# Two decoder layers in float32: gate and up by seven products of half size, and inner tiles in groups of six

## The chip, the core and the metric

The kernel runs on one core of one Trainium2 chip. A core has engines with an instruction queue each: TensorE (PE) multiplies matrices into banks of PSUM, of which this kernel uses eight, 128 x 512 numbers each; VectorE (DVE), ScalarE (ACT) and GpSimd (POOL) work on tiles of 128 partitions in on-chip memory (SBUF); SyncE (SP) issues the DMAs that bring data from HBM. Engines run side by side and wait for each other by semaphores. The metric is the time of one execution on the device in microseconds, the median of several runs.

## The reference

Two layers on x of 512 tokens by 1024, float32. Each layer is an FFN, a token mixer and an FFN:

```python
h = _rmsnorm(x) * (1.0 + sc1) + sh1
x = x + HALF_STEP * g1 * (jax.nn.silu(h @ w_gate) * (h @ w_up)) @ w_down
h = _rmsnorm(x) * (1.0 + sc2) + sh2
x = x + g2 * _hybrid_mixer(h, w_in[l], w_out[l], ...)
h = _rmsnorm(x) * (1.0 + sc3) + sh3
x = x + HALF_STEP * g3 * _swiglu(h, ffn2 weights)
```

`w_gate` and `w_up` are 1024 x 2816, `w_down` is 2816 x 1024. The shifts, scales and gates (sh, sc, g) are nine rows per layer, `SiLU(c) W_mod + b_mod`: one token's vector times 1024 x 9216 weights. The mixer has projections (1024 x 3584), three kinds of attention and an output projection; the change leaves its arithmetic alone.

## The kernel before, in words

**Layout and precision.** Everything is held transposed: features in partitions, the 512 tokens in columns. A block is 128 features; h has 8 blocks (`ND`), the inner width 22 tiles (`NF`). The products run on operands of the type fp32r. Each operand is split exactly into two parts of 12 bits, a high part (a cast on ScalarE) and a low part (VectorE subtracts the cast from the original), and each product is three matmuls, high x high, high x low, low x high: `triple` (L742). Matmuls add up in a PSUM bank over the blocks.

**FFN** (`ffn`, L848). Inner tiles go in groups of 8, 8 and 6 (L851). In a group they go by pairs: one load of 1 MB holds the 1024 x 256 weights of gate for two tiles, the next those of up. For each tile `dense` (L818) runs 8 blocks x 3 parts = 24 matmuls of 512 columns into one bank. ScalarE takes SiLU of a gate's bank (`gate_out`), VectorE multiplies by the up bank, and the result is split into high and low hidden rows (`up_out`). After the group's last tile come its down products (`down`, L911): for each of 8 output blocks, the group's inner tiles x 3 matmuls, added to x by VectorE (`residual`). The first pair of an FFN runs half the tokens at a time (`first`, L825), because h comes in halves from `norm` (L748). The first FFN's first pair has a hand-written order (`opening`, L338). At the end of an FFN the last four output blocks also go in halves.

**Weights** (`feed`, L703). `plan` (L603) lists all loads in order; SP's queue issues each as soon as one of three buffers (`RAW`) is free. A weight load is split by two casts and two subtractions of 128 x 1024 elements into the pools `WH` and `WL`, two of each. Among the weights, `plan` puts 64 loads of modulation weights, 1 MB each: one or two after each pair of tiles, one after each load of down weights. VectorE multiplies and adds them up (`background`, L645: two operations of 1024 elements per load, and a reduction after every fourth).

**Order.** The order in each engine's queue is fixed when the program is built. Streams of steps (main, feed, background, one per bank to be emptied) are merged by `Flow` (L143): of all steps that may run, the one goes next that a plain model of the engines would start first, with small biases. Slots of SBUF and banks are handed out in that order. The banks are in two pools, `M` (2) and `B` (6). Every instruction is recorded through one helper (L104), so the profile shows nearly all under that line and is read by the tiles' names: `m` and `a` are the banks of `M` and `B`, `w` a loaded buffer, `wh` and `wl` its parts, `hh` and `hl` the parts of h, `u` any of the 42 slots, `x` the residual stream, `acc` the modulation's sums.

Of the kernel before, what the change touches and what calls it, by code (L numbers as in the profile page):

```python
# [11 lines left out]
F32 = mybir.dt.float32  # L12
# [81 lines left out]
class Engine:  # L94
    """An engine that tells the Flow what each instruction reads, writes and about takes."""
# [19 lines left out]
class Pool:  # L115
    """Slots of one tag: how many are held, and about when each free one was last used."""
# [15 lines left out]


class Step:
    """What a stream does next: on which engine, after which tiles, with how many new slots."""
# [7 lines left out]
class Flow:  # L143
    """Emits streams of instructions (generators of Steps) merged into one program order.

    Of all streams whose next step may run, the one goes first that a plain model of the engines
    would start first; between equals the one of the higher rank.
    """
# [4 lines left out]
    def __init__(self):  # L153
        self.clk = dict.fromkeys(("PE", "ACT", "DVE", "POOL", "SP"), 0.0)
        self.ready, self.used, self.writer, self.owner = {}, {}, {}, {}
        self.streams, self.serial = [], 0
# [21 lines left out]

    def account(self, eng, op, out, ins):
        if eng == "SP":  # L180
# [3 lines left out]
            n = out.tensor.name  # L184
            start = max(self.clk["SP"], 0.0 if self.writer.get(n) == "SP" else self.ready.get(n, 0.0))
            self.clk["SP"] = start + size / 350e3
            end = self.clk["SP"] + 2.0
        else:
            t = self.clk[eng]
            for a in [out, *ins]:  # L190
                n = a.tensor.name
                if a.space != bass.MemoryType.DRAM and self.writer.get(n) != eng:
                    t = max(t, self.ready.get(n, 0.0))
# [3 lines left out]
        for a in ins:  # L197
            self.used[a.tensor.name] = max(self.used.get(a.tensor.name, 0.0), end)
        n = out.tensor.name
        self.used[n] = max(self.used.get(n, 0.0), end)  # L200
        if eng == "PE":
            end = max(end, self.ready.get(n, 0.0))
        self.ready[n] = end
        self.writer[n] = eng
# [16 lines left out]
    def start(self, s):  # L221
# [3 lines left out]
        for pool, n in st.need:  # L225
            if len(pool.free_at) < n + st.spare:
                return None
        t = self.clk[st.engine] if st.engine != "SP" else self.clk["PE"]
        late = self.MARGIN if st.engine == "PE" and s[0] == 0 else LATE if st.engine == "PE" and s[0] == 4 else 0.0
        for a in st.deps:  # L230
            t = max(t, self.ready.get(a.tensor.name, 0.0) + late)
# [22 lines left out]
def trunk(ctx, tc, x, c, w_mod, b_mod, f1g, f1u, f1d, w_in, w_out, qng, kng, hng, lbl, f2g, f2u, f2d, cf, out):  # L254
# [13 lines left out]
    U = Pool(F, space("up", UNITS), "u", [P, S], UNITS)  # L268
    RW = Pool(F, space("wraw", RAW), "w", [P, 8, 256], RAW)
    WH = Pool(F, space("whi", SPLIT), "wh", [P, 8, 256], SPLIT)  # L270
    WL = Pool(F, space("wlo", SPLIT), "wl", [P, 8, 256], SPLIT)
    HH = Pool(F, space("hhi", ND), "hh", [P, S], ND)
    HL = Pool(F, space("hlo", ND), "hl", [P, S], ND)
# [64 lines left out]
    def opening():  # L338
        """Up to the products of the first tiles of gate and up, in a fixed order.

        Layer 0's first shift and scale come 256 columns of each at a time, and are followed by the
        products of the two rows of h that they give.
        """
        hs = [(HH.get(F32R), HL.get(F32R)) for _ in range(ND)]
# [49 lines left out]
        def row_sums(e, n):  # L394
            """The first n rows' share of the modulation, on the tensor engine."""
# [38 lines left out]
        tmp = [U.get() for _ in range(3)]  # L434

        def modulate(d):
            hi, lo = hs[d]
            t = tmp[d % 3]
# [8 lines left out]
        def products(which, ds):  # L447
            for d in ds:
                for i in range(2):
                    w, o = ws[which], slice(i * P, (i + 1) * P)  # L450
                    triple(outs[2 * which + i], w[0][:, d, o], w[1][:, d, o], *hs[d], d == 0, d == ND - 1)

        def split(r, engine):
            hi, lo = WH.get(F32R), WL.get(F32R)
            ws.append((hi, lo))
            for h in range(2):
                cs = slice(h * P, (h + 1) * P)
                A.copy(hi[:, :, cs], r[:, :, cs])
                engine.tensor_sub(lo[:, :, cs], r[:, :, cs], hi[:, :, cs])
# [33 lines left out]
        U.put(junk, *tmp)  # L493
# [4 lines left out]
        return hs, outs  # L498
# [37 lines left out]
    def lower_bounds():  # L536
        """Of both layers side by side: [lower bound of layer 0 | of layer 1], four columns each."""
# [38 lines left out]
        # near 1 the logarithm is 2 atanh((v - 1) / (v + 1))  # L576
# [24 lines left out]
    MODS = [(0, j) for j in (2, 4, 3, 5, 7, 6, 8)] + [(1, j) for j in (1, 0, 2, 4, 3, 5, 7, 6, 8)]  # L601

    def plan():  # L603
# [6 lines left out]
        def through(l, j):  # L610
            """All modulation up to the one named."""
# [3 lines left out]
        for l in range(DEPTH):  # L615
            for wg, wu, wd, last in ((f1g, f1u, f1d, 0), (f2g, f2u, f2d, 1)):
                for f0 in range(0, NF, 8):
                    n = min(8, NF - f0)
# [939 lines left out]
```

## Time and profile before

| | before |
|---|---|
| median of 3 runs | 2170.38 us (2168.68 to 2173.84) |
| profiled execution, its span | 2173.2 us |
| TensorE busy | 2127.0 us, 98% |
| weight loads into TensorE busy | 1809.0 us, 83% |
| VectorE busy | 1237.3 us, 57% |
| ScalarE busy | 808.6 us, 37% |
| GpSimd busy | 177.9 us, 8% |
| DMA | 259.06 MB, 119 GB/s mean |

The profile is of one execution. Its span, from the first to the last instruction, is what it gives of that execution's own time. A group's row gives line, engine, operation, tile written <- tiles read, shape and count, then busy time and mean duration in ns, then the engine's idle time before it and what ended that. Busy time is the union of instructions, so where they overlap at their ends it counts once, while the mean is of whole durations. A timeline row gives start, length, and how many instructions of a kind were merged into it (x2). Pieces of the chain of work that ended last are given as start, length, engine and tile, count. The two layers show as FFN 0 (to about 380 us), mixer, FFN 1 (from about 745), FFN 2 (from about 1108), mixer, FFN 3 (from about 1808).

### The profile page before, as it was taken

The numbers are of one execution on the slowest core, as the hardware profiler recorded it, in microseconds if no ns is written. First come the engines' busy times: TensorE is split into PE (matmuls) and PEld (weight loads), VectorE is DVE, ScalarE is ACT, GpSimd is POOL, SyncE is SP. The second block draws the span as 40 slices with busy tenths as digits, with TensorE's granted clock in tenths as the row PEclk, the third lists the DMA queues.
The fourth block names the chain that finished last, engine by engine and source line by source line (L and its number), as shares of the span: only waits on it lengthen the run. The fifth ranks groups of instructions, "written<-read, shape, count | busy, mean of one in ns | idle before, by whom it ended". The sixth has DMA issues, their size and how long they took to land.

```text
span 2173.2 us, 26686 instructions
## 1 busy us (share of the span) xinstructions
PE 2127.0 (98%) x10936; PEld 1809.0 (83%) x10936; DVE 1237.3 (57%) x1874; ACT 808.6 (37%) x1272; POOL 177.9 (8%) x219
## 2 busy tenths in 40 slices
PE   7999999999999999999999999999999999999999
PEld 6888888988887888888898888888878788888887
DVE  5765554675678665455475546447766866333333
ACT  3332222465655432222342222236464644222221
POOL 3000000140320100000000000003013201000000
PEclk7999999999999999999999999999989999999999
DMA  8555453221111155454335545432101113223221
GB/s 293 187 205 194 155 174 117 97 79 59 50 42 65 59 190 190 135 173 152 130 103 170 180 150 174 150 102 98 59 26 62 49 59 117 97 97 97 97 83 54
DMA packets 206625, 259.06 MB, mean 119 GB/s; under 512 B 4927, under 2 KB 188186, under 8 KB 206504
## 3 DMA queue, kind: packets, MB, share of 16 engines
q1 hardware_dynamic: 206472, 257.33, 35.3%
q8 instruction: 86, 1.41, 0.3%
q14 instruction: 35, 0.29, 0.0%
q0 software_dynamic: 32, 0.04, 0.0%
HBM read 255.25 MB, written 2.10 MB: 118 GB/s over the span
## 4 chain that ended last, share of the span: by engine, by line
PE 93%; DVE 4%; ACT 1%; issue 1%; DMA 0%; POOL 0%; SPq 0%; POOLq 0%; DVEq 0%; ACTq 0%
PE m L104 59%; PE a L104 34%; DVE wl L104 1%; DVE u L104 1%; ACT u L104 1%; DVE hl L104 1%; DVE acc L104 1%; ACT wh L104 0%; DVE x L104 0%; DMA u<-in_x_dram 0%; POOL u L104 0%; SPq L104 0%; ACT hh L104 0%; ACT L104 0%; ACT x L104 0%
## 5 line engine op out<-in xcount | busy, mean ns | idle before, releaser
L104 ACT CAST wh<-w 128x1024 fp32r<-128x1024 f32 (+1 forms) x348 | 344.8, 1018 | 744.8 <-PE m L104 542.8
L104 DVE TENSOR_TENSOR wl<-w,wh 128x1024 fp32r<-128x1024 f32 (+1 forms) x346 | 416.0, 1225 | 253.7 <-ACT wh L104 250.1
L104 PE MATMUL m<-u,wh 128*128 128x512 f32 (+1 forms) x1808 | 514.7, 370 | 3.6 <-DVE u L104 2.3
L104 PE MATMUL m<-hh,wh 128*128 128x512 f32 (+1 forms) x1072 | 415.3, 387 | 4.2 <-DVE x L104 4.1
L104 PE MATMUL m<-hl,wh 128*128 128x512 f32 (+1 forms) x1072 | 406.0, 379 | 2.5 <-DVE hl L104 2.4
L104 PE MATMUL m<-hh,wl 128*128 128x512 f32 (+1 forms) x1072 | 405.6, 378 | 0.5 <-DVE wl L104 0.5
L104 PEld LDWEIGHTS m<-u,wh 128*128 128x128 f32 x1808 | 324.1, 189 | 60.7 <-DVE u L104 3.6
L104 PE MATMUL m<-u,wl 128*128 128x512 f32 (+1 forms) x904 | 331.4, 367 | 0.0
L104 PE MATMUL a<-hh,wh 128*128 128x512 f32 (+1 forms) x816 | 302.6, 371 | 0.0
L104 PE MATMUL a<-hh,wl 128*128 128x512 f32 (+1 forms) x816 | 302.3, 370 | 0.1
L104 PE MATMUL a<-hl,wh 128*128 128x512 f32 (+1 forms) x816 | 301.9, 370 | 0.0
L104 PEld LDWEIGHTS m<-hh,wh 128*128 128x128 f32 x1072 | 206.6, 193 | 38.9 <-ACT u L104 4.6
L104 PEld LDWEIGHTS m<-hl,wh 128*128 128x128 f32 x1072 | 206.3, 192 | 37.9 <-DVE hl L104 3.9
L104 PEld LDWEIGHTS m<-hh,wl 128*128 128x128 f32 x1072 | 205.4, 192 | 38.5 <-DVE wl L104 1.4
L104 POOL TENSOR_TENSOR u<-u 128x256 f32<-128x256 f32 x162 | 126.2, 806 | 1260.4 <-ACT u L104 1246.5
L104 DVE SCALAR_TENSOR_TENSOR x<-m,mod,x 128x512 f32<-128x512 f32 (+1 forms) x136 | 91.0, 671 | 212.1 <-PE m L104 212.0
L104 DVE TENSOR_TENSOR u<-u 128x256 f32<-128x256 f32 (+3 forms) x324 | 185.6, 593 | 37.9 <-ACT u L104 34.7
L104 PEld LDWEIGHTS m<-u,wl 128*128 128x128 f32 x904 | 171.0, 189 | 28.1
L104 PEld LDWEIGHTS a<-hh,wl 128*128 128x128 f32 x816 | 154.7, 190 | 26.5 <-DVE wl L104 0.3
L104 PEld LDWEIGHTS a<-hl,wh 128*128 128x128 f32 x816 | 154.7, 190 | 25.8
L104 PEld LDWEIGHTS a<-hh,wh 128*128 128x128 f32 x816 | 154.5, 189 | 25.6
L104 DVE TENSOR_TENSOR u<-u,a 128x512 f32<-128x512 f32 x88 | 60.2, 687 | 196.7 <-PE a L104 196.0
(132 smaller groups left out, 2054.4 us busy)
## 6 DMA issues: line engine op xcount, KB each, us to landing
w<-in_w_mod_dram SPq DMA_DIRECT2D x64, 1024.0 KB, 4.7
w<-in_ffn_w_gate_dram SPq DMA_DIRECT2D x44, 1024.0 KB, 5.2
w<-in_ffn_w_up_dram SPq DMA_DIRECT2D x44, 1024.0 KB, 5.2
w<-in_ffn_w_down_dram SPq DMA_DIRECT2D x32, 1024.0 KB, 5.1
w<-in_w_in_dram SPq DMA_DIRECT2D x28, 1024.0 KB, 5.0
w<-in_ffn_w_down_dram SPq DMA_DIRECT2D x16, 768.0 KB, 5.3
u<-in_w_mod_dram SPq DMA_DIRECT2D x32, 256.0 KB, 6.6
w<-in_w_out_dram SPq DMA_DIRECT2D x8, 512.0 KB, 4.0
```

The source lines that it names most:

```text
L104: ins = fn(*args, **kw)
```

## The change

Gate and up of nine pairs of tiles in each FFN (tiles 4 to 21; the first two pairs stay as they were) are computed by a scheme with seven products where the plain one has eight. The work of one load, 1024 x 256 weights times 1024 x 512 of h, is cut in two each way: the blocks of h into 4 and 4, the 256 columns into two tiles, the tokens into two halves. Each of the seven products is 4 blocks x 3 parts of 256 columns. Their operands are quarters of h and of the weights, and sums of such quarters.

- `feed` makes the weights' sums from a load of kind "f": four additions of 128 x 512 elements in place, then four parts a, b, c, d (1024, 512, 1024 and 1024 elements) cast and subtracted. They take 7 slots of 4 KB, out of 11 that weights may hold (`HELD`); 4 slots are a plain load's share.
- `combine` makes the sums of h once per FFN from values that `norm` keeps: per block, four operations of 256 elements, two casts and two subtractions of 512.
- `seven` issues the products into three banks. Four of them go to the first bank and add up on what it holds; ScalarE copies the bank's state out between them (`empty`), VectorE does three operations of 256 elements. SiLU and the product with up are then taken in halves for one tile of the pair, whole for the other (`gate_seven`, `up_seven`).
- Groups are of 6, 6, 6 and 4 inner tiles, so there are four rounds of down products and of adding to x, not three; modulation loads come after every second load of down weights.
- Slots: one pool of 37 slots of 4 KB (`Slots`), whole or as two halves of one type, serves h, weights and all else, in place of separate pools. Plain loads are split by blocks (0 to 3, 4 to 7), not by columns.
- `Flow` follows halves of a slot apart.

The core of the diff (comments and docstrings also go):

```diff
-UNITS = 42
+SLOTS = 37
 RESERVE = 4
 RAW = 3
-SPLIT = 2
+HELD = (11, 8)
+GROUP = 6
+FAST = (tuple(range(4, NF, 2)),) * 4
...
                         if f or not (l or last):
                             yield from take(2 if f < TWO[2 * l + last] else 1)
...
-                        yield from take(1 if n == 8 else 0)
+                        yield from take(1 if n == GROUP and dd % 4 == 0 else 0)
...
+            elif item[0] == "f":
+                w = {}
+                r0, r1 = r[:, 0:4], r[:, 4:8]
+                c0, c1 = slice(0, P), slice(P, 2 * P)
+                yield Step("ACT", r, need=((WS, 2),), bias=haste())
+                w["a"] = hi, lo = [WS.get().rearrange("p (k f) -> p k f", f=P) for _ in range(2)]
+                A.copy(hi, r[:, :, c0])
...
+                A.copy(b[:, 0], r1[:, :, c1])
...
+                V.tensor_sub(lo, r[:, :, c0], hi)
...
+                V.tensor_add(r0[:, :, c0], r0[:, :, c0], r0[:, :, c1])
...
+                V.tensor_sub(b[:, 1], r1[:, :, c1], b[:, 0])
...
+                V.tensor_add(r0[:, :, c1], r0[:, :, c1], r1[:, :, c1])
+                for n, rr in (("c", r0), ("d", r1)):
+                    yield Step("ACT", r, need=((WS, 2),), bias=haste())
+                    w[n] = hi, lo = [WS.get().rearrange("p (k f) -> p k f", f=256) for _ in range(2)]
+                    A.copy(hi, rr)
+                    if n == "c":
+                        yield Step("DVE", r, bias=haste())
+                        V.tensor_add(r1[:, :, c1], r0[:, :, c0], r1[:, :, c1])
+                        yield Step("DVE", r, bias=haste())
+                        V.tensor_add(r1[:, :, c0], r1[:, :, c1], r1[:, :, c0])
+                    yield Step("DVE", hi, bias=haste())
+                    V.tensor_sub(lo, rr, hi)
...
+    QUARTER = {"w11": ("a", 0, 0), "w21": ("a", 4, 0), "w22": ("b", 0, 0), "t1": ("c", 0, 0), "t3": ("c", 0, P),
+               "t4": ("d", 0, 0), "t2": ("d", 0, P)}
+    def seven(w, hs, sums, banks, uid):
...
+        for n, a, q, bank, begin, after, free in (
+                (1, (0, 0), "w11", 0, True, (), ""), (5, "x5", "t1", 2, True, (), ""), (6, "x6", "t2", 0, False, ("s1",), ""),
+                (2, (0, 1), "w21", 1, True, (), "a"), (7, "x7", "t3", 0, False, ("s2",), "c"),
+                (3, "x3", "w22", 2, False, ("s5",), "b"), (4, (1, 1), "t4", 0, False, ("s7",), "d")):
+            if after:
+                yield when(*((uid, z) for z in after))
+            ps = banks[bank][:, :HALF]
+            for k in range(4):
+                wh, wl = quarter(q, k)
+                xh, xl = rows(a, k)
+                yield Step("PE", xl, wh, wl)
+                triple(ps, wh, wl, xh, xl, begin and k == 0, k == 3, True)
...
+    def empty(banks, uid, fin):
...
+        A.copy(e0[:, lo], b0)
+        done.add((uid, "s1"))
...
+        A.copy(e1[:, hi], b2)
+        done.add((uid, "s5"))
...
+        A.copy(e1[:, lo], b0)
+        done.add((uid, "s2"))
...
+        V.tensor_add(e0[:, lo], e0[:, lo], b1)
...
+        A.copy(e0[:, hi], b0)
+        done.add((uid, "s7"))
...
+        V.tensor_sub(e1[:, hi], e1[:, hi], e0[:, hi])
...
+        V.tensor_sub(e1[:, lo], b2, e1[:, lo])
...
+                if f in fast:
+                    yield when((phase, "sums"))
+                    for name, pools, fin in (("g", (M, M, B), gate_seven), ("u", (B, B, B), up_seven)):
+                        w = yield from next_weight()
+                        yield Step("PE", need=tuple((p, pools.count(p)) for p in (M, B) if p in pools))
+                        banks = [p.get() for p in pools]
+                        uid = (phase, name, f)
+                        F.spawn(empty(banks, uid, fin(f)), 0)
+                        yield from seven(w, hs, sums[phase], banks, uid)
```

More of the change, by code (lines that the diff above doesn't have):

```diff
@@ L131, in put, with room, __init__, whole @@
             heapq.heappush(self.free_at, self.flow.used.get(t.tensor.name, 0.0))
+    def room(self, n, spare):
+        return len(self.free_at) >= n + spare
+class Slots:
+    def __init__(self, flow, pool, n):
+        self.flow, self.pool, self.free_at = flow, pool, [0.0] * n
+        self.open = {F32: [], F32R: []}
+        self.parents = {}
+    def whole(self, dt=F32R):
+        t0 = heapq.heappop(self.free_at)
+        t = self.pool.tile([P, 2 * S], dt, tag="u", name="u")
+        n = t.tensor.name
+        self.parents[n] = t
+        self.flow.halved.add(n)
+        for i in range(2):
+            self.flow.ready[n, i] = t0
+        return t
+    def get(self, dt=F32):
+        if self.open[dt]:
+            self.open[dt].sort(key=lambda h: h[0])
+            _, t, i = self.open[dt].pop(0)
+            self.flow.ready[t.tensor.name, i] = max(self.flow.ready[t.tensor.name, i], self.flow.used.get((t.tensor.name, i), 0.0))
+        else:
+            t, i = self.whole(dt), 0
+            self.open[dt].append((self.flow.ready[t.tensor.name, 1], t, 1))
+        return t[:, i * S:(i + 1) * S]
+    def pair(self):
+        t = self.whole()
+        return t[:, :S], t[:, S:]
+    def put(self, *tiles):
+        for t in tiles:
+            n, used = t.tensor.name, self.flow.used
+            for k in self.flow.keys(t):
+                i = k[1]
+                spot = self.open[t.dtype]
+                other = [h for h in spot if h[1].tensor.name == n]
+                if other:
+                    spot.remove(other[0])
+                    heapq.heappush(self.free_at, max(used.get((n, 0), 0.0), used.get((n, 1), 0.0)))
+                else:
+                    spot.append((used.get(k, 0.0), self.parents[n], i))
+    def room(self, n, spare):
+        one = len(self.open[F32]) if n == 1 else 0
+        n += spare
+        return 2 * len(self.free_at) + one >= n + (n % 2 if not one else 0)
+class Held:
+    def __init__(self, slots, most):
+        self.slots, self.most, self.n = slots, most, 0
+    def get(self):
+        self.n += 1
+        return self.slots.whole()
+    def put(self, *tiles):
+        self.n -= len(tiles)
+        self.slots.put(*tiles)
+    def room(self, n, spare):
+        return self.n + n <= self.most and len(self.slots.free_at) >= n + spare
 class Step:
@@ L177, in cost, with keys @@
         return 0.0
+    def keys(self, a):
+        n = a.tensor.name
+        if n not in self.halved:
+            return (n,)
+        o = a.offset % (2 * S)
+        e = o + sum(step * (count - 1) for step, count in list(a.ap)[1:])
+        return tuple((n, i) for i in range(o // S, e // S + 1))
     def account(self, eng, op, out, ins):
@@ L225, in start @@
         for pool, n in st.need:
-            if len(pool.free_at) < n + st.spare:
+            if not pool.room(n, st.spare):
                 return None
@@ L738, in release, with part @@
     def release(w):
-        WH.put(w[0])
-        WL.put(w[1])
-    def triple(ps, wh, wl, xh, xl, start, stop):
-        T.matmul(ps, wh, xh, start=start, stop=False)
-        T.matmul(ps, wh, xl, start=False, stop=False)
-        T.matmul(ps, wl, xh, start=False, stop=stop)
-    def norm(phase, l, jsh, t, hs, order):
+        for parts in w:
+            WS.put(*parts)
+    def part(w, k, i=None):
+        o = slice(0, 256) if i is None else slice(i * P, (i + 1) * P)
+        return tuple(z[:, k % 4, o] for z in w[k // 4])
```

310 lines of the change are left out of this document (226 added, 84 removed).

## The prediction

> **What bounds the kernel now.** Read first: the page's busy times, then its slices, then the chain of work that ended last.
>
> ```profile
> span 2173.2 us, 26686 instructions
> PE 2127.0 (98%) x10936; PEld 1809.0 (83%) x10936; DVE 1237.3 (57%) x1874; ACT 808.6 (37%) x1272; POOL 177.9 (8%) x219
> DVE  5765554675678665455475546447766866333333
> PEclk7999999999999999999999999999989999999999
> PE 93%; DVE 4%; ACT 1%; issue 1%; DMA 0%; POOL 0%; SPq 0%; POOLq 0%; DVEq 0%; ACTq 0%
> ```
>
> Matmul ends are modelled, so 98% alone proves little; but 93% of the chain lies on TensorE, its granted clock is full outside the opening, and only 46 us of the span (2173.2 - 2127.0) show no matmul. TensorE is the bound nearly everywhere. VectorE is next: 50 to 80% busy in most slices, 30% in the last FFN.
>
> What a matmul costs is read from pieces of the chain (start, duration, count) where nothing but matmuls stands:
>
> ```profile
> 895.44 10.88 PE m L104 x48
> 752.80 5.76 PE m L104 x48
> ```
>
> The first is one weight load's work, a pair of tiles of a gate: 2 tiles x 8 blocks x 3 parts = 48 matmuls of 512 columns, 10.88 / 48 = 227 ns each. The second is the start of a phase, where half the tokens go at a time: 256 columns, 5.76 / 48 = 120 ns each. Every matmul has its own weight load in both. Half the columns cost 53% of the time.
>
> **The products.** Per weight load the change replaces 48 x 227 ns = 10.88 us by 7 products x 4 blocks x 3 parts = 84 x 120 ns = 10.08 us: 0.80 us less. There are 9 pairs x 2 (gate, up) x 4 FFNs = 72 such loads, all on the path: **-57.6 us**.
>
> The Trainium skill (TensorE: Matmul & The Clock Gate, "Back-to-back issue gap") puts the gap at N/2.4 + 2.5 ns, 109 and 216 ns here, by which this term would be an estimated -86 us. The trace's 120 and 227 ns differ from it by some 11 ns on either, which is lost on every half-width matmul, and they decide.
>
> **What VectorE gets for it.** Its prices, from pairs that run back to back and from groups:
>
> ```profile
> 918.14 2.36 DVE L104 TENSOR_TENSOR wl<-w,wh 128x1024 fp32r<-128x1024 f32 x2 [0.21 <-ACT wh L104]
> 1826.55 1.28 DVE L104 TENSOR_TENSOR u<-u,a 128x512 f32<-128x512 f32 x2
> 469.42 0.74 DVE L104 TENSOR_TENSOR u<-u 128x256 f32<-128x256 f32 x2
> 899.56 2.60 DVE L104 SCALAR_TENSOR_TENSOR acc<-w,sc_c,acc 128x1024 f32<-128x1024 f32 x2
> L104 DVE TENSOR_TENSOR wl<-w,wh 128x1024 fp32r<-128x1024 f32 x298 | 368.5, 1261 | 229.0 <-ACT wh L104 225.4
> L104 DVE TENSOR_TENSOR u<-u,a 128x512 f32<-128x512 f32 x88 | 60.2, 687 | 196.7 <-PE a L104 196.0 <-ACT u L104 0.7
> L104 DVE SCALAR_TENSOR_TENSOR acc<-w,sc_c,acc 128x1024 f32<-128x1024 f32 x112 | 143.5, 1281 | 2.0
> L104 DVE TRANSPOSE_TENSOR_REDUCE p<-acc 128x32 f32<-128x1024 f32 x16 | 19.9, 1244 | 0.5
> L104 DVE SCALAR_TENSOR_TENSOR mod<-a,bcol 32x8 f32<-32x8 f32 x64 | 10.3, 161 | 24.1 <-PE a L104 23.4
> ```
>
> Instructions overlap at their ends: a second one adds 2.36 - 1.26 = 1.10 us (1024 elements), 1.28 - 0.69 = 0.59 (512), 2.60 - 1.28 = 1.32 (modulation's sum); for 256 I take half a pair, 0.37. Per pair of tiles:
> - Splitting a load: two subtractions (2.2 us) become three of 1024, one of 512 and four additions of 512: 3 x 1.10 + 5 x 0.59 = 6.25. Gate and up: 12.5.
> - Emptying the banks: new, three operations of 256 per load, 2 x 3 x 0.37 = 2.2.
> - Multiplying by up, splitting the hidden rows: 0.59 + 2 x 0.37 + 2 x 0.59 = 2.5.
>
> That is 17.2 us against TensorE's 2 x 10.08 = 20.16. A modulation load adds 2 x 1.32 + (1.24 + 4 x 0.16) / 4 = 3.1. With one per pair, VectorE needs 20.3 us of 20.16. It is not yet the bound, because work can be done ahead. A full group of three pairs with three modulation loads needs 51.6 + 9.3, and 1.7 for the first down weights: 62.6. While the group before ends, one whole load (6.25) and the first part of the next (1.10 + 3 x 0.59 = 2.9) fit into the 11 slots; about 2 us fall behind the group's end. That leaves 51.5 of 60.5 us, 85%; in FFN 0's second group, with five modulation loads, 57.7, 95%. The down products give the room ahead:
>
> ```profile
> 829.90:873.40 43.50, 43.50 (x194) 36.01 (x194) 24.51 (x28) 8.37 (x9) 0.00 (x0) 1.00 0.56 188
> 1826.80:2160.00 333.20, 333.20 (x1483) 275.76 (x1482) 124.92 (x140) 85.08 (x105) 0.00 (x0) 1.00 0.29 96
> L104 DVE SCALAR_TENSOR_TENSOR x<-m,mod,x 128x512 f32<-128x512 f32 x96 | 71.8, 751 | 191.7 <-PE m L104 191.6
> w<-in_w_mod_dram SPq DMA_DIRECT2D x64, 1024.0 KB, 4.7
> w<-in_ffn_w_gate_dram SPq DMA_DIRECT2D x44, 1024.0 KB, 5.2
> ```
>
> In a group's down products (columns of a window: length, then PE, PEld, DVE, ACT, POOL) VectorE works 24.5 of 43.5 us. With six inner tiles they take 32.7 us, need 8 x 0.75 for residuals, 4 x 1.7 for weights and two modulation loads, 19 us, and leave 13 free for the 9.1 above. The last FFN, at 125 of 333 us, has room everywhere. Two more things I cost at nothing: the 8 residuals more per FFN (6 us, in those 13; uncovered, 24 in all) and the sums of x (4 blocks x (4 x 0.37 + 2 x 0.59) = 11 us per FFN), which have the first two pairs, 43 us, before their first use (uncovered, 44 in all). On SP's queue the modulation loads move: two per group of down weights, not four. Each issue waits for a free buffer, with the next weights behind it. A buffer is now held for the length of a load's products, 10 us: two loads of 5.2 + 10 and one of 4.7 + 3 are 38 of the 3 x 20 us that three buffers offer per pair, so the queue keeps up; with two modulation loads 46.
>
> I still expect weights to come late at times. Part c of the next load gets its slots when 4 of the 7 products of this one are done, at 5.8 us; a cast (1.0, half of the row of 2.01 below), two additions and a subtraction make 9.1, and it is asked for at 10.1 + 1.44 = 11.5. Part d follows at 10.2 for 13.0. So 2.4 us are spare, and a modulation step (1.32) with one subtraction (1.10) in the way uses them. I take 0.2 us for each of the 54 loads in the first three FFNs: **+11**, bounds 0 and the second rival.
>
> **Ends of groups.** The last product now finishes both tiles, so hidden tile k = n - 2 is late where it was one tile (5.4 us) early.
>
> ```profile
> L104 PE MATMUL a<-hl,wh 128*128 128x256 f32 x160 | 45.3, 283 | 0.0
> L104 DVE TENSOR_TENSOR u<-u 128x256 f32<-128x256 f32 x132 | 56.9, 468 | 6.8 <-ACT u L104 6.8
> L104 ACT CAST u<-u 128x512 fp32r<-128x512 f32 x102 | 62.9, 618 | 157.9 <-DVE u L104 157.7
> L104 DVE TENSOR_TENSOR u<-u 128x512 fp32r<-128x512 f32 x136 | 95.7, 709 | 29.0 <-ACT u L104 27.2 <-POOL u L104 1.2
> ```
>
> From the last matmul's start: 0.28 + 0.37 + 0.47 (two halves multiplied) + 0.62 + 0.71 = 2.45 us. The down products ask for that tile after 0.12 + 4 x 3 x 0.227 = 2.84 us in a group of six, after 1.48 in the last group of four. With nothing in the queues: 12 groups at 0, 4 at 1.0. With two weight subtractions in the way (2.2): 12 x 1.8 + 4 x 3.2 = 34. I take half a one at each of two steps: 12 x 0.6 + 4 x 1.5 = **+13**, bounds 4 and 34.
>
> **Bank reuse.** Four products add up in one bank, which ScalarE reads in between; one product on another bank, 12 x 0.120 = 1.44 us, covers each read.
>
> ```profile
> 301.30 2.01 ACT L104 CAST wh<-w 128x1024 fp32r<-128x1024 f32 x2 [9.15 <-PE m L104]
> L104 ACT COPY u<-m 128x256 f32<-128x256 f32 x8 | 3.0, 374 | 8.6 <-PE m L104 8.3
> ```
>
> 0.28 + 0.37 = 0.65 us of 1.56 (with the last matmul's own 0.12); one cast in the way (about 1.0) just uses the rest. **+4** for 216 reads, bounds 0 and the third rival. Opening, mixers and changes of phase keep their work; the new order and pool of slots may move their 46 us without matmuls by -5 to +8; I take 0.
>
> **Sum:** -57.6 + 11 + 13 + 4 = -29.6: 2173.2 becomes 2143.6 in the profiled execution, which was 2.8 above the median of 2170.4; by the median **2141 us**, with its own bounds at 2120 and 2160.
>
> **Rivals.**
> 1. *Everything stays covered.* VectorE's 85% with 9 us done ahead speaks for it, the 95% group against. Only the four short groups cost 4: 2170.4 - 57.6 + 4 = 2117, to 2112 with what the mixers may give.
> 2. *Slower: VectorE's order holds the gate and up stage.* Before, a group of three pairs took 3 x 21.76 = 65.3 us; VectorE needs 51.5. If waits between it and ScalarE let it use less than 51.5 / 65.3 = 79% of the stage, the group loses. For it: no FFN slice of before shows VectorE at 80%. Against: it idled then because it had nothing to do. At 75% a group lasts 68.7 (+3.4), that with five loads 76.9 (+11.6); with the short groups at +1: FFN 0 +16, the next two +8 each, the last FFN -12: +20, 2190; at 70% 2230.
> 3. *Bank reads held up.* Two casts ahead of a copy cost 0.65 + 2.0 - 1.56 = 1.1 us; at every fifth of 216 reads 47 us, so -57.6 + 13 + 47: 2173, no change. For it: per load, casts and copies go from 2.0 to 3 x 1.0 + 0.62 + 4 x 0.37 = 5.1 of 10.1 us, and a cast that waits for a slot or for VectorE holds every copy queued behind it, and so TensorE. Against: that is still half. The Trainium skill (Perfetto Trace Analysis, "Matmuls") advises rotating independent groups through banks and larger matmuls; this change goes against both, and no row of before shows the cost.
> 4. *TensorE's own weight loads lie open,* 36 more of them per load of 1 MB:
>
> ```profile
> L104 PEld LDWEIGHTS a<-hh,wl 128*128 128x128 f32 x816 | 154.7, 190 | 26.5 <-DVE wl L104 0.3
> ```
>
> At 190 ns a matmul 84 x 0.190 = 16.0 us, 72 x 5.1 = 367 us slower, 2537. The 120 ns above, loads included, speak against it. The Trainium skill (TensorE: Matmul & The Clock Gate, "The mechanism") lets a load overlap running matmuls only where row groups differ; the trace disagrees, by 120 against 190 ns.
>
> **How the numbers follow.** Forecast 0.56, first rival 0.19, second 0.16, third 0.08, fourth 0.01. Two runs of this kernel can be told apart from about 0.2%, 4.3 us. Faster: 0.56 + 0.19 + 0.01 of the third = 0.76; same: 0.05 of it; slower: 0.19. The range runs from the first rival into the second, 2114 to 2186; some 0.06 lies below and 0.12 above.
>
> **What would show it.** Right: matmul pieces of x84 or so at 10.1 us in the gates and ups of all FFNs; VectorE about 85 to 95% in the first three FFNs' gate and up; TensorE's gaps 1 us long, at the starts of down products, and behind the splitting of weights where modulation runs; the last FFN shorter by some 10 us. Wrong: 256 columns at other than 120 ns; TensorE idle 2 us and more per load behind VectorE (second rival) or behind ScalarE's copies (third); a mixer that is longer.

## The result, and the profile after

The changed kernel takes 2220.68 us (median of 4 runs, 2218.92 to 2222.76) where the kernel before takes 2169.53 beside it: a ratio of 1.0225, with a 95% interval of 1.0206 to 1.0243. It is slower by 2.2%; the forecast was faster, 2141 us. In the profiled executions the span goes from 2173.2 to 2221.0 us, +47.8.

From the page of the kernel after: its span, the engines' busy times, the slices of VectorE and of the granted TensorE clock, and the chain that ended last.

```profile
span 2221.0 us, 33173 instructions
...
PE 2101.4 (95%) x13456; PEld 1896.7 (85%) x13456; DVE 1679.5 (76%) x2694; ACT 1048.2 (47%) x1797; POOL 191.7 (9%) x221
...
DVE  6778788678558787878878778878755878776765
...
PEclk7889999999899999999999999999999999999999
...
PE 82%; DVE 11%; DMA 3%; ACT 2%; issue 1%; SPq 0%; ACTq 0%; DVEq 0%
```

There are more matmuls (13456, before 10936), and TensorE's busy time falls by 25.6 us where the products alone should have given 57.6, so the other matmul time grew by 32 us. About 20 of them are the clock: TensorE is busy for 116 us of stretches with a granted clock of 0.5, before for 76, and half of such a stretch is lost (summed over both traces). The other 12 I can't put down to one cause. The time without a matmul grows from 46.2 to 119.6 us (2221.0 - 2101.4). So +47.8 is -57.6, +32.0 of other matmul time and +73.4 without any. VectorE's share of the chain rises from 4% to 11%.

Where this lies is seen in windows cut at the same places of the two kernels' FFNs (length; busy time and count of PE, PEld, DVE, ACT, POOL; granted clock, DMA share, GB/s). First the kernel before, FFN 0, 1 and 3:

```profile
0.00:439.40 439.40, 420.72 (x2021) 356.65 (x2022) 260.35 (x366) 144.28 (x211) 26.09 (x25) 0.96 0.52 176
...
764.20:1131.70 367.50, 365.16 (x1768) 309.41 (x1767) 198.95 (x242) 108.67 (x150) 7.66 (x10) 1.00 0.45 152
...
1826.70:2173.20 346.50, 341.68 (x1524) 282.38 (x1522) 128.59 (x145) 85.12 (x105) 0.00 (x0) 1.00 0.29 94
```

The kernel after, FFN 0, 1 and 3:

```profile
0.00:491.30 491.30, 426.46 (x2642) 386.12 (x2643) 367.48 (x566) 205.32 (x343) 29.24 (x26) 0.91 0.47 155
...
816.80:1186.70 369.90, 356.61 (x2390) 328.67 (x2389) 304.00 (x447) 168.00 (x281) 8.86 (x10) 0.99 0.44 143
...
1874.80:2221.00 346.20, 332.26 (x2172) 303.74 (x2170) 241.53 (x347) 138.99 (x229) 0.00 (x0) 0.98 0.32 101
```

FFN 0 with the opening is 51.9 us longer, FFN 1 2.4 longer, FFN 2 0.5 and FFN 3 0.3 shorter; by the sum each should have been 6 to 10 us shorter. (The mixers make up the rest: +0.7 and -6.4.) The clock fell in FFN 0 above all, from 0.96 to 0.91.

The products themselves do what was forecast. From the chain of the kernel after, in FFN 3 (start, length, what):

```profile
1990.50 10.08 PE a L109 x84
...
2010.66 10.09 PE a L109 x84
...
2020.77 0.43 DVE u L109 x2
...
2021.45 2.52 DVE u L109 x3
...
2024.01 1.19 PE m L109 x4
```

84 matmuls take 10.08 us, one load's work. Behind the last of a group the chain goes over VectorE to the last hidden tile, 3.3 us later, while TensorE has down products of the other tiles to do: this group's down products take only 0.6 us more than their matmuls. Where modulation runs, the same 504 matmuls of a group (six loads) look like this, in windows of the kernel after: FFN 0's second and third group, FFN 1's third, and FFN 3's second for comparison.

```profile
178.60:252.30 73.70, 66.65 (x509) 65.25 (x508) 55.93 (x81) 33.38 (x58) 0.00 (x0) 0.93 0.38 126
285.40:354.30 68.90, 64.20 (x508) 62.95 (x508) 60.38 (x87) 33.65 (x61) 0.00 (x0) 0.95 0.45 148
990.60:1060.10 69.50, 64.46 (x508) 63.32 (x507) 60.42 (x87) 33.65 (x61) 0.00 (x0) 0.95 0.45 147
1960.10:2020.60 60.50, 60.50 (x506) 60.50 (x505) 46.75 (x70) 32.92 (x60) 0.00 (x0) 1.00 0.28 89
```

The last row is the ideal, 60.5 us with TensorE busy throughout, VectorE 46.75. The third groups of FFN 0 and FFN 1 took 69 us, and VectorE has 60.4 us of work in them, as much as TensorE would have needed. The second group of FFN 0 took 73.7 with VectorE at work for only 55.9. That looks like another cause, and the rows behind it show which. DMA issues of SP there, then VectorE, then TensorE (start, length, what, idle before it and what ended that):

```profile
190.05 0.37 SPq L109 DMA_DIRECT2D w<-in_ffn_w_up_dram  x1
192.69 10.10 SPq L109 DMA_DIRECT2D w<-in_w_mod_dram  x2
210.84 0.37 SPq L109 DMA_DIRECT2D w<-in_ffn_w_gate_dram  x1
```

```profile
209.59 1.22 DVE L109 TENSOR_TENSOR u<-w,u 128x1024 fp32r<-128x1024 f32 x1
...
216.90 0.42 DVE L109 TENSOR_TENSOR u<-u,a 128x256 f32<-128x256 f32 x1 [4.49 <-PE a L109]
217.24 1.28 DVE L109 SCALAR_TENSOR_TENSOR acc<-w,sc_c,acc 128x1024 f32<-128x1024 f32 x1
...
233.45 1.28 DVE L109 SCALAR_TENSOR_TENSOR acc<-w,sc_c,acc 128x1024 f32<-128x1024 f32 x1
```

```profile
223.91 0.50 PE L109 MATMUL a<-u 128*128 128x256 f32 x2 [1.36 <-ACT u L109]
226.11 2.50 PE L109 MATMUL a<-u 128*128 128x256 f32 x10 [1.70 <-DVE u L109]
```

Three buffers take loads. At 202.8 two hold modulation's loads (the second row is two issues, the last at 202.42) and one an up load. The next gate's load has to wait until the split of that up load ends at 209.59 + 1.22 = 210.81; it is issued at 210.84. VectorE meanwhile idles for 4.49 us, until a bank of TensorE is ready; the first sum of the load issued at 192.69, which had long landed (5.1 us by the median of its queue), stands behind that in VectorE's order and runs at 217.24, the second at 233.45. So this load keeps a buffer for 42 us. When the gate is there, its split starts late, and TensorE waits 1.36 and 1.70 us for its parts. From issue to the end of its second sum, where it gives up the buffer, a modulation load takes 18.6 us before and 31.1 us after (mean of the 64 loads, each issue of SP with the pair of sums on `acc` that belongs to it, in the order of both); the prediction had 4.7 + 3.

The start of FFN 3's down products shows what TensorE makes of it. VectorE, then TensorE:

```profile
1924.35 1.83 DVE L109 TENSOR_TENSOR u<-w,u 128x1024 fp32r<-128x1024 f32 x2 [1.35 <-ACT u L109]
1926.10 2.60 DVE L109 SCALAR_TENSOR_TENSOR acc<-w,sc_c,acc 128x1024 f32<-128x1024 f32 x2
1928.73 1.25 DVE L109 TRANSPOSE_TENSOR_REDUCE p<-acc 128x32 f32<-128x1024 f32 x1
```

```profile
1930.03 0.63 PE L109 MATMUL a<-p,quads 128*128 128x32 f32 x2 [4.78 <-DVE p L109]
1932.62 9.74 PE L109 MATMUL m<-u 128*128 128x512 f32 x29 [1.95 <-DVE x L109]
```

Modulation's last sums stand between the splits of down weights that came late, and TensorE, whose queue holds modulation's closing product (`p`, `quads`), waits 4.78 us for it and 1.95 us for x behind it. Then it is slow for a while, as windows behind the gap show:

```profile
1932.60:1939.30 6.70, 6.68 (x17) 5.26 (x18) 0.53 (x1) 0.55 (x2) 0.00 (x0) 0.54 0.18 55
1939.30:1942.50 3.20, 3.20 (x16) 2.63 (x15) 2.58 (x4) 0.00 (x0) 0.00 (x0) 1.00 0.05 7
```

17 matmuls of 512 columns take 6.7 us at a granted clock of 0.54, the next 16 take 3.2 us at 1.00. The starts of the slow ones are 427 ns apart, of the others 227.

### The profile page after: what moved, and what is told of

The parts are those of the page before. It is cut to its first block, busy times and chain, and to the rows that moved or that the text cites. A ratio compares the mean times of both kernels' runs of the same rounds, so it can differ in the third digit from the quotient of the medians.

```text
span 2221.0 us, 33173 instructions
## 1 busy us (share of the span) xinstructions
PE 2101.4 (95%) x13456; PEld 1896.7 (85%) x13456; DVE 1679.5 (76%) x2694; ACT 1048.2 (47%) x1797; POOL 191.7 (9%) x221
## 4 chain that ended last, share of the span: by engine, by line
PE 82%; DVE 11%; DMA 3%; ACT 2%; issue 1%; SPq 0%; ACTq 0%; DVEq 0%
PE m L109 49%; PE a L109 33%; DVE u L109 8%; ACT u L109 2%; DVE w L109 1%; DVE acc L109 1%; DMA w<-in_ffn_w_down_dram 1%; DVE x L109 1%; DMA w<-in_ffn_w_gate_dram 1%; DMA w<-in_w_in_dram 1%; DMA u<-in_x_dram 0%; SPq L109 0%; DVE lbw L109 0%; DMA u<-in_k_norm_g_dram 0%; DVE mod L109 0%
## 5 line engine op out<-in xcount | busy, mean ns | idle before, releaser
L109 PE MATMUL m<-u 128*128 128x256 f32 (+1 forms) x7056 | 1300.7, 340 | 58.8 <-ACT u L109 32.6
L109 PEld LDWEIGHTS m<-u 128*128 128x128 f32 x7056 | 1088.7, 194 | 211.7 <-ACT u L109 41.5
L109 PE MATMUL a<-u 128*128 128x256 f32 (+6 forms) x5832 | 802.4, 293 | 23.5 <-DVE u L109 17.0
L109 PEld LDWEIGHTS a<-u 128*128 128x128 f32 (+1 forms) x5832 | 754.1, 194 | 57.7 <-DVE u L109 20.5
L109 DVE TENSOR_TENSOR u<-w,u 128x1024 fp32r<-128x1024 f32 x506 | 546.8, 1097 | 98.9 <-ACT u L109 97.6
L109 ACT CAST u<-w 128x1024 fp32r<-128x1024 f32 x508 | 460.5, 940 | 323.6 <-DVE w L109 142.2
L109 DVE TENSOR_TENSOR u<-u 128x256 f32<-128x256 f32 (+3 forms) x536 | 303.5, 585 | 37.9 <-ACT u L109 33.9
L109 DVE TENSOR_TENSOR w<-w 128x512 f32<-128x512 f32 x288 | 198.0, 688 | 4.5
L109 ACT ACTIVATE u<-u 128x512 f32<-128x512 f32 (+2 forms) x290 | 155.3, 563 | 36.5 <-POOL u L109 26.0
L109 DVE SCALAR_TENSOR_TENSOR acc<-w,sc_c,acc 128x1024 f32<-128x1024 f32 x112 | 144.3, 1288 | 2.0
```

Of the source, the lines that this page charges most:

```text
L109: ins = fn(*args, **kw)
```

## The experiments

Three theories. **V**: VectorE has too much to do where modulation runs beside the split of seven products. **L**: loads come late, since modulation's loads hold the three buffers and SP's queue passes the wait on. **S**: the new groups and slots cost by themselves. Each kernel is the changed one with the edit shown; times are medians, ratios are to the kernel before, run beside it, with 95% intervals. "After" stands for the changed kernel's 2221.

**No seven products** (groups of 6 and slots stay; the sums of h are not made where they have no use, here and in the next):

```diff
-FAST = (tuple(range(4, NF, 2)),) * 4
+FAST = ((),) * 4
```

> All pairs by eight products again (none of the loads takes seven, no sums of h or of weights); groups of 6, the new slots and the new places of the modulation loads stay. Theory V (VectorE has too much to do while modulation runs) and theory L (loaded buffers are held too long, so loads land late): both need the seven products, so this is near the kernel before, 2165 to 2180, with FFN 0 as long as before within 5 us. Theory S (groups, slots and places of loads cost by themselves): 2195 or more.

2179.4 us, ratio 1.0028 (1.0011 to 1.0045). S costs about 6 us and not the rest. In its trace FFN 0 is longer than before by 14 us, where the expectation allowed 5, and the mixers are shorter by 7.

**Seven products in FFN 1 to 3 only:**

```diff
-FAST = (tuple(range(4, NF, 2)),) * 4
+FAST = ((),) + (tuple(range(4, NF, 2)),) * 3
```

> Only FFN 0 goes back to eight products; the other three keep seven. V and L: the 51 us that FFN 0 lost go, the rest stays: 2165 to 2175. S: FFN 0 keeps at least half of its loss, 2195 or more. My forecast's own sum (each FFN gains) would give 2150.

2176.8 us, ratio 1.0021 (1.0003 to 1.0038), 2 above the range of V and L. 44 us of the loss are FFN 0's. The stalls of FFN 1 to 3 stay where they were, each within 2 us (9.1 us in FFN 1's third group, 7.3 in FFN 2's down products), so what FFN 0 does late is not handed on.

**Half of modulation's sums** (one of each pair is left out, so the modulation's values are half sums):

```diff
-            for k in range(2):
+            for k in range(1):
```

> Of each modulation load only the first of its two rows of blocks is multiplied and added (half of the modulation's sums is left out); everything else as changed. VectorE loses 64 x 1.3 = 83 us of work, and each buffer of modulation is free some us earlier. V: the waits inside the gates and ups of FFN 0 and 1 (30 and 12 us) go nearly all, and of the starts of down products (54) most: 2150 or less. L: the waits for loads shrink by a third, 2195 to 2210.

2168.8 us, ratio 0.9978 (0.9965 to 0.9992): 52 us off after, for 82 us of VectorE's work (1679.5 to 1597.4). That lies between the ranges of V and L, and both allow it: the sums give the buffers back earlier too (a modulation load keeps its buffer for 22.9 us in the mean, after for 31.1). FFN 0's second group keeps 11.2 us of its stall.

**Four buffers** at the cost of two slots, and later its control with three:

```diff
-SLOTS = 37
-RESERVE = 4
-RAW = 3
+SLOTS = 35
+RESERVE = 6
+RAW = 4
```

> Four buffers for loads in place of three, paid with two slots (35, not 37) and a reserve of 6 slots in the mixer, not 4. VectorE's work is the same. L: the long waits at starts of down products (13.6, 10.4 and 4.8 us) and that of 11 us in FFN 0's second pair go: 2175 to 2190. V: within 8 us of 2221.

> Control for the run with a fourth buffer: 35 slots, a reserve of 6 and three buffers. If the fourth buffer was worth something that the two lost slots took back (L), this is slower than that run's 2225, by 10 us or more. If it is at 2220 to 2228, the fourth buffer gave nothing by itself.

2225.4 us, ratio 1.0251 (1.0216 to 1.0286), and 2229.1, ratio 1.0267 (1.0246 to 1.0288), for the control. The intervals overlap; the fourth buffer is worth 4 us at most by the medians. With four buffers a modulation load keeps its own for 50.2 us in the mean, with three and the same slots for 31.1: the fourth buffer lets a load come earlier and wait longer. More room for loads isn't what is missing, as a count.

**Two of the four additions of a split on GpSimd:**

```diff
-                yield Step("DVE", r, bias=haste())
-                V.tensor_add(r0[:, :, c0], r0[:, :, c0], r0[:, :, c1])
+                yield Step("POOL", r, bias=haste())
+                G.tensor_add(r0[:, :, c0], r0[:, :, c0], r0[:, :, c1])
...
```

> Two of the four additions of a load's weights go from VectorE to GpSimd (8% busy): 72 x 2 x 0.59 = 85 us of work taken from VectorE, as much as in the run with half of the modulation, but no buffer is free earlier; GpSimd takes about 1.6 us for one. V (VectorE's load is the cause): 2165 to 2185. L (buffers are held too long): 2220 or more, since a buffer is held longer still.

2219.4 us, ratio 1.0214 (1.0164 to 1.0265): nothing. But it wasn't the test of V that it was meant to be. The groups of GpSimd and of VectorE in this run, then of VectorE after:

```profile
L109 POOL TENSOR_TENSOR w<-w 128x512 f32<-128x512 f32 x144 | 221.2, 1536 | 1119.4 <-DVE u L109 1064.4 <-DMA w<-in_ffn_w_up_dram 49.3
```

```profile
L109 DVE TENSOR_TENSOR u<-u 128x512 f32<-128x512 f32 x68 | 66.5, 979 | 1.3
```

```profile
L109 DVE TENSOR_TENSOR w<-w 128x512 f32<-128x512 f32 x288 | 198.0, 688 | 4.5
...
L109 DVE TENSOR_TENSOR u<-u 128x512 f32<-128x512 f32 x68 | 46.9, 689 | 1.4
```

An addition takes 1.54 us on GpSimd where VectorE's back-to-back step is 0.6, and it stands in the chain of the split; VectorE's operations of 512 elements with both inputs in SBUF, the product with up among them, grow from 689 to 979 ns in the mean. One by one, the 19 of these 68 that ran while GpSimd added took 1722 ns, the other 49 took 690. So 85 us were to go from VectorE, and its busy time falls by only 41 (1679.5 to 1638.3). The Trainium skill (SBUF — State Buffer, "Who interferes with whom") has VectorE's operations with two inputs in SBUF and GpSimd's reads contend for a shared port; the 1722 ns beside 690 agree.

**Constants for the mixer asked for later** (`late`):

```diff
-        yield when((0, "hid", 3))
+        yield when((0, "hid", 11))
```

> The small loads of constants and their two transpositions on TensorE begin after hidden tile 11, not 3; nothing else. If the 11 us gap at 91 us is TensorE's queue standing behind those transpositions, which wait for loads: 2205 to 2212. If VectorE's backlog makes that gap and only shows there, it moves elsewhere: within 4 us of 2221.

2212.9 us, ratio 1.0185 (1.0128 to 1.0241), 8 off after. The 16.9 us stall at FFN 0's first down products goes, and most of it comes back in its third group (8.4 to 16.4) and last group (2.7 to 8.3). The gap at 91 us, which the edit was to remove, stays: without a wait for constants TensorE stands still there for 11.28 us, now before modulation's closing product, while VectorE does six of modulation's sums in a row (rows of VectorE and TensorE; "issue" means that the profile shows nothing that ended the wait):

```profile
95.24 7.88 DVE L109 SCALAR_TENSOR_TENSOR acc<-w,sc_c,acc 128x1024 f32<-128x1024 f32 x6
```

```profile
104.50 0.61 PE L109 MATMUL a<-p,quads 128*128 128x32 f32 x2 [11.28 <-issue]
```

So the constants weren't what TensorE lacked there: VectorE begins its part of the next gate's split at 102.64 in the kernel after and at 104.63 here.

**The same modulation loads, spread:** one at a pair of tiles at most, and one behind each projection of the mixer.

```diff
-TWO = (10, 6, 4, 4)
+TWO = (0, 0, 0, 0)
...
-                        yield from through(l + last, 0 if last else 6)
+                        yield from through(l + last, 0 if last else 3)
...
                     yield ("w", [(0, w_in[l, :, c0:c0 + 256], ND, 256)])
+                    yield from take(1)
```

> Modulation loads are spread: one after each pair at most (FFN 0 had two after five of its pairs), one after each projection of the mixer; FFN 0 has 17 and not 24, FFN 3 none. VectorE's total work is the same. V: the waits of FFN 0's gates and ups fall from 30 to under 10 us, FFN 3's wait of 10.7 at its first down products goes, mixers gain no more than 10: 2180 to 2195. If the total of VectorE's work counts and not its place: 2215 or more.

2171.2 us, ratio 0.9998 (0.9979 to 1.0017): 50 off after and 9 below V's range, with VectorE's work the same to 0.1% (1678.4 us busy). So the total of VectorE's work isn't what holds it up; where it falls is, or where the loads stand, which move with it. In this run FFN 0's second group and FFN 2's third:

```profile
159.10:221.00 61.90, 61.18 (x506) 60.63 (x505) 52.21 (x75) 32.93 (x58) 0.00 (x0) 1.00 0.44 145
...
1312.60:1378.20 65.60, 63.13 (x508) 62.39 (x507) 56.61 (x84) 33.30 (x60) 0.00 (x0) 0.97 0.44 141
```

With VectorE at 52 us a group takes 62, close to the ideal; the longest in this run is that with the most for VectorE, 56.6 us, at 65.6.

**FFN 0 plain, spread, and constants later:** the edits of three runs above together.

> FFN 0 by eight products, modulation spread as in the run before, constants later. V: FFN 0 loses at most 5 us to the kernel before, the other three gain 8 to 12 each where modulation no longer crowds VectorE, mixers within 5: 2140 to 2155, faster than both kernels. L: the waits at starts of down products stay (2.6, 7.3, 8.7, 5.8): 2165 or more.

2156.7 us, ratio 0.9918 (0.9885 to 0.9951): 0.8% under the kernel before, and clear of the noise.

**Two additions of each split left out** (the weights' sums of four of the seven products then lack them, not of five as the expectation has it):

```diff
-                yield Step("DVE", r, bias=haste())
-                V.tensor_add(r0[:, :, c0], r0[:, :, c0], r0[:, :, c1])
...
-                yield Step("DVE", r, bias=haste())
-                V.tensor_add(r0[:, :, c1], r0[:, :, c1], r1[:, :, c1])
```

> Leaves out the first two of the four additions of 512 in each of the 72 splits (so the right factors of five products are wrong; every product, cast and subtraction stays). It takes 72 x 2 x 0.59 = 85 us of VectorE's work away, unlike the run with these additions on GpSimd without a slower engine in the chain of the split. Theory V (VectorE has too much work between the loads): most of the excess in the gates and ups of the first three FFNs goes, 2165 to 2185. Theory L (loaded buffers are held too long and modulation's loads stand in SP's queue): little changes, 2205 to 2222.

2174.8 us, ratio 1.0017 (1.0003 to 1.0030): 46 off after, as V had it. It doesn't exclude L: a modulation load keeps its buffer for 26.9 us in the mean, not 31.1. The same work on GpSimd gave nothing; without it FFN 0's second and third group and FFN 1's third are

```profile
172.50:234.30 61.80, 61.02 (x506) 60.60 (x505) 48.16 (x67) 32.88 (x58) 0.00 (x0) 1.00 0.46 153
269.00:332.70 63.70, 61.45 (x507) 60.82 (x506) 50.43 (x73) 33.82 (x60) 0.00 (x0) 1.00 0.40 129
...
954.90:1015.60 60.70, 60.70 (x507) 60.66 (x507) 47.80 (x72) 31.26 (x58) 0.00 (x0) 1.00 0.42 137
```

**Modulation without its loads** (VectorE does every sum on the accumulator itself, so modulation's weights are left out):

```diff
     def load(i):
+        if items[i][0] == "mod":
+            return None
...
-                    V.scalar_tensor_tensor(acc, rv[:, k], s, acc, ALU.mult, ALU.add)
-            RW.put(r)
+                    V.scalar_tensor_tensor(acc, acc, s, acc, ALU.mult, ALU.add)
...
```

> Modulation's 56 loads are left out with their buffers; VectorE does every one of modulation's sums as before, on the accumulator itself, and all operations of the splits (so the modulation's values are wrong). VectorE's work is that of the changed kernel to within 1%. Theory L: the loads' gaps go with the buffers that they held: 2160 to 2185. Theory V: 2210 to 2225, since VectorE has as much to do at the same places.

2191.5 us, ratio 1.0098 (1.0083 to 1.0113): 29 off, between the two theories. All 64 loads of 1 MB are gone, not 56 as the expectation has it. The full groups of gate and up have no stall left (the third pair of FFN 0 keeps 6.8 us), but TensorE waits for `p`, modulation's closing product, as a row of its waits shows (us, times, longest):

```profile
PE a L109 <- DVE p L109: 39.4, 5, 12.7
```

So that product was put later, behind 6 us of planned work of TensorE, once in this kernel and once in the changed one alone:

```diff
+                yield lambda: F.stuck or F.clk["PE"] > F.ready[part.tensor.name] + 6.0
                 yield Step("PE", part, need=((B, 1),), bias=0.0)
```

(`stuck` is set when no other step may run.)

> As the run without modulation's loads (the modulation's values are wrong in the same way), and modulation's closing product is put into TensorE's order 6 us later than its operand is planned. Theory L (modulation's loads take buffers and the queue; VectorE's work is no limit by itself): the 39 us of waits for p go, 2150 to 2165, that is 55 to 70 below the changed kernel with VectorE's work unchanged. Theory V: the waits return at other places, since VectorE is as late, 2180 to 2195.

2167.9 us, ratio 0.9982 (0.9971 to 0.9994): 53 off after, 3 us above L's range. The waits for `p` are halved, not gone:

```profile
PE a L109 <- DVE p L109: 20.4, 3, 12.7
```

Windows of this run: FFN 0's second and third group, FFN 1's third.

```profile
167.80:228.50 60.70, 60.70 (x508) 60.70 (x507) 52.59 (x81) 34.09 (x61) 0.00 (x0) 1.00 0.29 90
262.00:322.50 60.50, 60.50 (x506) 60.49 (x505) 52.96 (x77) 32.87 (x60) 0.00 (x0) 1.00 0.29 90
...
952.20:1012.60 60.40, 60.40 (x505) 60.40 (x504) 51.34 (x76) 32.61 (x60) 0.00 (x0) 1.00 0.29 89
```

VectorE is busy 85 to 88% of each of them, its total is 1676.4 us, and TensorE never waits there. But these two runs don't leave VectorE's work in its place, as their expectations have it. A sum that waits for no load goes elsewhere in the order: 3, 4 and 2 of modulation's sums fall into these three groups, where the kernel after has 8 in each, and in the two third groups VectorE's work falls from 60.4 to 53.0 and 51.3 us. So they can't tell L from V.

> The changed kernel with modulation's closing products later, nothing else. Its trace shows 5.6 us of waits for p, so 2212 to 2218 if these go and nothing else moves; 2221 or more if VectorE's lateness only shows elsewhere.

2239.2 us, ratio 1.0312 (1.0297 to 1.0327): 18 slower than after. Closing products that come later let modulation's values come later, and TensorE then waits at `x` (16.0 us in all, after 6.0) and in FFN 2's groups (5.3 and 8.2 us, after 1.6 each).

**All four FFNs, spread, and constants later:**

> Seven products in all four FFNs, modulation's loads spread (one per pair of tiles and one behind each projection of the mixer), late constants after tile 11. The parts gave -50 and -8 apart. If they add up, 2155 to 2165, below the kernel before; FFN 0's opening gap of 8 to 11 us stays, so about equal to the run that leaves FFN 0 with eight products (2157). If spreading alone had already removed the stalls that the later constants remove, 2168 to 2172.

2173.9 us, ratio 1.0012 (0.9999 to 1.0025). The two edits don't add up, and it isn't that one had taken what the other took: FFN 0's first down products stall for 16.9 us after, for 14.4 with the loads spread, not at all with the constants later, and for 12.8 with both. Its third group now stalls for 7.9 us.

**Modulation where VectorE has room.** FFN 0 plain, with two modulation loads at each of its pairs (first run) or its first five (second); else as the spread run, constants and closing products later.

```diff
-TWO = (10, 6, 4, 4)
+TWO = (22, 0, 0, 0)
```

> FFN 0 with eight products and two modulation loads at each of its pairs, where VectorE has room; one at each pair and projection behind that until none is left; late constants after tile 11; closing products later. FFN 1 to 3 keep seven products. If the loss is the crowding of modulation into stages with seven products, FFN 1 and 2 lose less than the 24 us that they keep in the run with FFN 0 plain and spread (2157): 2140 to 2152. If FFN 0 itself is then crowded, 2157 or more.

> As the run before, with two modulation loads only at FFN 0's first five pairs: between it and the run with one at each pair, 2143 to 2157.

2148.9 us, ratio 0.9899 (0.9883 to 0.9916), the fastest of all, 1.0% under the kernel before; and 2182.8, ratio 1.0050 (1.0034 to 1.0065), against its expectation. The page of the faster one:

```profile
span 2144.0 us, 31508 instructions
...
PE 2083.2 (97%) x12808; PEld 1856.0 (87%) x12808; DVE 1572.0 (73%) x2499; ACT 989.6 (46%) x1670; POOL 190.4 (9%) x223
...
PE 90%; DVE 7%; DMA 1%; ACT 1%; issue 1%; SPq 0%; DVEq 0%; ACTq 0%
```

The first mixer of the slower one is 31 us longer. Its longest stall is at one place, where five of modulation's sums come in a row on VectorE before their buffers are free; the projection's load behind them is issued at 674.51, ScalarE waits 9 us for it, and TensorE stands still for 11.5 us (rows of VectorE and ScalarE):

```profile
673.21 6.56 DVE L109 SCALAR_TENSOR_TENSOR acc<-w,sc_c,acc 128x1024 f32<-128x1024 f32 x5
```

```profile
679.60 1.99 ACT L109 CAST u<-w 128x1024 fp32r<-128x1024 f32 x2 [9.01 <-DMA w<-in_w_in_dram]
```

## Why the prediction was wrong, step by step

- **The products**, -57.6: right. 84 matmuls take 10.08 us, and groups of 504 take 60.5.
- **Bank reuse**, +4: nothing was paid. In the run without modulation's loads and with the closing product later, groups of 504 with 18 such reads each have no gap.
- **Ends of groups**, +13: about right. Undisturbed groups of six end with 0.6 us too much at most, the short ones of FFN 0 to 2 with 1.5 to 3.8.
- **x-sums and residuals**, nothing: not contradicted; in the run without modulation's loads the gates and ups of FFN 1 to 3, which use the sums, have no wait left, and the down products of their later groups take 0.9 us too much at most.
- **Opening and mixers**, 0 (-5 to +8): the mixers gave 5.7 us (+0.7 and -6.4). FFN 0 lost about 9 by the end of its second pair: its first 102.7 us have 25.7 without a matmul, the first 102 us of before 16.3. TensorE's two waits for constants there, 4.5 and 5.5 us, are not the cause: the run with the constants later has the same gap of 11 us without them. The next gate comes late, so it belongs to the next step.
- **Late weights**, +11: this step failed. Its premise was that a buffer is held "4.7 + 3" us for modulation, "so the queue keeps up". The trace has 31.1, and 18.6 already in the kernel before, where it could have been read. In place of 11 us there are 46 inside gates and ups (slower matmuls included): 31 in FFN 0 (6.2, 13.2, 8.4, 2.7), 12 in FFN 1, 3 in FFN 2 and none in FFN 3. Late loads also hit the starts of down products (16.9, 2.6, 7.4 and 10.7 us in one group of each FFN, 38 in all), which no term had: in FFN 2 the down weights are issued at 1330.87, when a modulation load has just given up its buffer after 50.5 us, and TensorE waits 4.38 us for their split. And there are the 11 us of the gap at 91. These 95 us, the products' -57.6 and the mixers' -5.7 make +32 of the +47.8; the 16 us left are near the +13 of the ends of groups.
- **The clock** was taken as full outside the opening. Pauses of TensorE from about 2 us on are followed by half speed (last section), and about 20 us of the loss, already within the stalls above, are matmuls at that speed.
- **The second rival** had the sign and, at 2190 to 2230, the size, but its mechanism (VectorE can't use more than 75% of a stage) falls: in the run without modulation's loads and with the closing product later it uses 85 to 88% at no loss, and FFN 0 was to lose 16 and lost 52.

VectorE's prices were right in total: the prediction's terms add up to about 444 us more for VectorE (36 pairs of tiles at 17.2 us instead of 6.76, 44 for the sums of x, 24 for the residuals), and the trace has 442 (1679.5 - 1237.3). But within a group more of it falls than the sum had: 42.2 us for a group without modulation (51.5 - 9.3) against 46.75 in FFN 3. The operations counted in that window make 44.8 us at the sum's prices (my estimate); the rest of the difference is work that the sum put ahead of the group. With four modulation loads at 3.1 it is 59 of 60.5 us, near the 60.4 of the two 69 us groups.

What the runs show is a crowding in time. Cut VectorE's work by 5 to 6% and 46 to 52 us go; move the loads and leave the work, and 50 go; take the loads away, by which the sums move too, and 29 go, 53 with the closing product later. Over all traces here the full groups of 504 matmuls sort by the work that VectorE has in them: with 54 us or less a group takes at most 4.1 us more than 60.5 (two groups of the run with GpSimd apart, with 10.4 and 13.5), with 58 us or more it takes at least 8.2 more, and between them it varies from 1.1 to 13.2. A longer group also takes in more work, so this sorting by itself is no proof of the cause. The rows of FFN 0's second group show how the two theories meet: modulation's loads wait in buffers for sums that stand behind a split, the next gate comes late, VectorE idles and then has the group's work and modulation's at once. How the 77 us between forecast and result (2221.0 - 2143.6, both profiled executions) divide between VectorE's work and the buffers stays open, since each edit that gained much changed both. A mean hold of 34 us in the spread run, longer than after's, and of 50.2 with four buffers at nearly the control's time say that the hold by itself isn't the price, but what queues behind it. That a fourth buffer without the loss of slots would help wasn't tried.

## What to carry to other kernels

When a change gives an off-path engine a third more work (here from 57% to 76% of the span), its mean share doesn't tell the cost. Add up its work stage by stage, background work included (here 60.4 us in groups of 60.5); list the buffers that wait for this engine, measure before the change how long each is held (18.6 us here, not the 7.7 of load and sums), and see which load is issued next into them. Background work that was laid out beside an idle engine has to be laid out again: the same sums at other places were worth 50 us, nearly the 57.6 that the products gave. And where the trace shows the clock drop behind a gap, a gap on TensorE costs more than its length.

## What was new of the hardware

Half speed behind pauses: in the trace of the kernel after, matmuls of 512 columns start every 427 ns, not 227, behind TensorE's pause of 4.78 us. Much shorter pauses do it too. In the kernel before, at the change from FFN 1 to FFN 2, a pause of 2.34 us is followed by 3.4 us at a granted clock of 0.50 (a row of TensorE, then a window):

```profile
1106.67 0.75 PE L104 MATMUL a<-u,ones 128*128 128x256 f32 x2 [2.34 <-POOL u L104]
```

```profile
1107.20:1110.60 3.40, 3.40 (x17) 3.38 (x16) 3.40 (x7) 2.69 (x6) 0.00 (x0) 0.50 0.50 140
```

In the kernel after, two pauses of 1.36 and 1.70 us within 4 us were enough: the ten matmuls of 256 columns at 226.11, shown above, take 2.50 us, about twice their 120 ns each. And each of the drops that begin inside its FFNs behind the opening has at least 1.9 us without a matmul in the 3.4 us ahead of it. The matmuls then run slow for 3 to 11 us. The Trainium skill (TensorE: Matmul & The Clock Gate, "What's actually happening") has the clock at half after an idle window of about 3.4 us; the pause of 4.78 us agrees, the shorter ones don't, and here the measurement decides.

GpSimd's addition of 128 x 512 took 1536 ns in the mean beside 688 on VectorE. VectorE's own 68 operations of 512 elements with two inputs in SBUF (`u<-u` above) took 1722 ns where a GpSimd addition ran beside them and 690 where none did.
